# Experts of a routed layer: unsplit 4-byte products on column halves instead of three products of split parts

## The chip, the core and the metric

The kernel runs on one core of one Trainium2 chip. The time is that of one execution on the device in microseconds (us), and of several runs the median counts. One execution was recorded by the hardware profiler; all rows below are from it. TensorE multiplies matrices, ScalarE and VectorE work on elements, GpSimd works on elements more slowly and issues the indirect transfers (gathers and scatters by row), and SyncE issues the plain transfers. In rows, PE is TensorE, PEld its weight loads, ACT is ScalarE, DVE is VectorE, POOL is GpSimd, SP is SyncE; a q behind a name is that engine's sequencer.

## The reference

One layer of a decoder trunk on 1024 tokens of width 1024, all in 4-byte floats: a normalisation with a scale and shift made from a conditioning vector, one input projection, a gated linear recurrence in one branch, an attention over selected keys in the other, a gated merge and an output projection. The change touches what follows, a layer of routed experts:

```
g_sel = argmax(x @ w_group + b_group)                    # one of 4 groups
e_top = top 2 of 8 experts of that group
hid   = silu(xb @ w1[e]) * (xb @ w3[e])                  # 1024 -> 512
y     = hid @ w2[e]                                      # 512 -> 1024
out   = sum over the token's two experts of gate * y
```

Each of the 32 experts holds two 1024x512 weights and one 512x1024 weight, 6 MiB in all (6.29 MB). Every token goes to two experts, so an expert sees 64 tokens on the average, and how many it sees is known only while the kernel runs. The layer's result, scaled by a row, is added to the residual stream, and a last normalisation gives the output.

## The kernel before, in words

The trunk is one program in which stages follow one another: the input projection, the key selection, the recurrence, the attention, the merge, the output projection with the routing (`project_out`), and the experts (`experts`, `expert`, `combine`). Up to the experts nothing changes but two small tables.

Routing ends with a table of slots: for each expert a column of 128 slots in `idx`, which holds the tokens' row numbers, and a column of gates. Slots without a token hold a number out of bounds, which the gather and the scatter skip. An expert with more than 128 tokens would be finished by `overflow`, which runs under a condition that all engines evaluate (lines 1614 and 1618); with at most 128 tokens everywhere it is skipped.

In `expert` the 128 slots' rows are gathered, turned by eight transposes on TensorE (`tr`, line 1483), and split: `hilo` makes a rounded part with ScalarE and the rest with VectorE (lines 97 and 98). The weights are split likewise after they have landed (`weights`, lines 1472 and 1474). A product of two split operands is three one-pass products on TensorE, high by high, high by low and low by high: 48 of 128x512 for the first two weights (line 1501, into `pa` and `pb`), 24 for the third (`mm3`, lines 137 to 139, into `py`), 72 in all. Between them stand the activation (line 1506), the gated product (line 1507) and four transposes of the hidden layer. At the end the rows are scaled by the gate and the residual's scale (line 1539) and scattered with an addition onto the stream in memory (line 1543). The last two experts are not scattered; `combine` adds them by a product with a matrix of ones and zeros, and normalises.

The weights come as six transfers of 1 MiB per expert, which SyncE issues in order (line 1380) into a ring of buffers (`ring_tile`). Eight of the ring's buffers exist from the merge on, so some loads are early; five more (`ring_b`) are added for the first part of the experts and later given up to the overflow's memory. SyncE waits with each load until the last reader of its buffer is done; in this kernel the readers are the two engines that split. Two sets of buffers, six for high parts and four for low ones of 4 KiB per partition, hold the split weights.

The order of work is that of a list of generators: `experts` steps the generators of two neighbouring experts in turn, so that one expert's third product stands between the other's first products and its transposes; the framework then may order instructions of an engine by its own priorities.

## Time and profile before

| | us |
|---|---|
| median of 3 runs | 1864.37 |
| lowest and highest | 1861.35, 1865.53 |
| the profiled execution | 1865.06 |
| its span, first to last instruction | 1863.3 |

The mean granted clock of TensorE was 0.984 of full speed. Over the span TensorE was busy 1759.3 us, weight loads 1456.1, VectorE 1439.9, ScalarE 1170.1, GpSimd 398.8. The transfers moved 366.85 MB. The slices of the page divide the span by 40, 46.6 us each; a digit is the busy share in tenths. In the timeline a matmul's length goes from its start to a modelled end, and neighbours overlap; the distance from start to start is what one costs. In the groups by line, "idle before" is the time that the engine stood still ahead of such an instruction, with what ended it.

### The profile page before, as it was taken

Reading aid. Unit: us, or ns where it says so; the run is one execution under the profiler, and the core shown is the slowest. Engines: PE = TensorE matmul, PEld = TensorE weight load, DVE = VectorE, ACT = ScalarE, POOL = GpSimd, SP = SyncE. Lnnn points to the kernel's source line nnn. Section 1 sums busy time; section 2 is a strip of 40 time slices with the busy share of each in tenths; the row PEclk is TensorE's granted clock in tenths of the full one; section 3 lists DMA queues with packets and bytes.
Section 4 is the critical chain, followed back from the end, with each engine's and each line's share of the span. In section 5 each row is a group of like instructions: output and inputs, shape, how many; then the busy total and the mean of one; then the engine's idle time right before and its main releaser. Section 6 shows DMA issues by size and latency. Waiting matters only on the chain. (4 is left out here: it accounts for less than half of the span.)

```text
span 1863.3 us, 24597 instructions
## 1 busy us (share of the span) xinstructions
PE 1759.3 (94%) x8532; PEld 1456.1 (78%) x8532; DVE 1439.9 (77%) x2393; ACT 1170.1 (63%) x1730; POOL 398.8 (21%) x249
## 2 busy tenths in 40 slices
PE   3999999997999999999999999979999999999995
PEld 2788877786777888999788877858888888788774
DVE  6688876697777766778524456569999999999998
ACT  6565677725676767888512113348888887777765
POOL 4101002210010001212000001033554544344134
PEclk9999999998999999999999999979999999999998
DMA  9213754322112212121738544369989999999994
GB/s 297 61 35 104 237 179 147 109 89 65 59 54 73 68 58 93 55 66 57 216 107 252 194 152 170 138 238 350 379 329 344 363 376 367 366 380 371 357 338 182
DMA packets 163738, 366.85 MB, mean 197 GB/s; under 512 B 17855, under 2 KB 107543, under 8 KB 139160
## 3 DMA queue, kind: packets, MB, share of 16 engines
q1 hardware_dynamic: 152112, 340.50, 51.3%
q0 software_dynamic: 10192, 19.99, 3.9%
q10 hardware_dynamic: 1304, 4.74, 0.6%
q8 instruction: 68, 1.11, 0.3%
q14 instruction: 62, 0.51, 0.1%
HBM read 326.90 MB, written 54.53 MB: 205 GB/s over the span
## 5 line engine op out<-in xcount | busy, mean ns | idle before, releaser
L1472 ACT ACTIVATE whi<-raw_w 128x1024 fp32r<-128x1024 f32 x384 | 395.6, 1057 | 107.8 <-DMA raw_w<-in_moe_w_dram 28.2
L1474 DVE TENSOR_TENSOR wlo<-raw_w,whi 128x1024 fp32r<-128x1024 f32 x382 | 447.9, 1220 | 13.1 <-ACT whi L1472 4.7
L139 PE MATMUL pj<-uhi,wlo_in 128*128 128x512 f32 (+2 forms) x784 | 302.8, 387 | 5.6 <-POOL wlo_in L128 4.2
L137 PE MATMUL pj<-uhi,whi_in 128*128 128x512 f32 (+2 forms) x784 | 304.3, 388 | 1.2 <-ACT gq L706 1.2
L138 PE MATMUL pj<-ulo,whi_in 128*128 128x512 f32 (+2 forms) x784 | 302.0, 385 | 0.0
L1543 POOL DMA_INDIRECT h_spill<-ye,idx x30 | 179.4, 5980 | 215.0 <-DVE ye L1539 202.2
L139 PEld LDWEIGHTS pj<-uhi,wlo_in 128*128 128x128 f32 (+1 forms) x784 | 146.4, 187 | 37.8 <-POOL wlo_in L128 6.4
L137 PEld LDWEIGHTS pj<-uhi,whi_in 128*128 128x128 f32 (+1 forms) x784 | 146.6, 187 | 32.1 <-ACT gq L706 2.4
L138 PEld LDWEIGHTS pj<-ulo,whi_in 128*128 128x128 f32 (+1 forms) x784 | 146.6, 187 | 29.9 <-issue 1.0
L654 ACT ACTIVATE junk_a<-B,nt 128x768 bf16<-128x768 f32 (+2 forms) x93 | 96.8, 1041 | 49.6 <-DVE nt L650 41.2
L1501 PE MATMUL pa<-whi,xh 128*128 128x512 f32 x256 | 103.3, 403 | 0.6 <-ACT xh L97 0.5
L138 PE MATMUL py<-wlo,hh 128*128 128x512 f32 x256 | 100.9, 394 | 2.7 <-DVE wlo L1474 2.7
L1501 PE MATMUL pa<-whi,xl 128*128 128x512 f32 x256 | 100.6, 393 | 0.5 <-DVE xl L98 0.5
L137 PE MATMUL py<-gh,whi_y 128*128 128x512 f32 x256 | 99.9, 395 | 1.1 <-ACT gh L97 1.1
L1501 PE MATMUL pb<-whi,xh 128*128 128x512 f32 x256 | 100.0, 391 | 0.4 <-ACTq L1618 0.4
L139 PE MATMUL py<-gh,wlo_y 128*128 128x512 f32 x256 | 100.4, 393 | 0.0
L138 PE MATMUL py<-gl,whi_y 128*128 128x512 f32 x256 | 100.2, 393 | 0.1
L139 PE MATMUL py<-whi,hl 128*128 128x512 f32 x256 | 100.0, 391 | 0.0
L137 PE MATMUL py<-whi,hh 128*128 128x512 f32 x256 | 99.8, 400 | 0.1
L1501 PE MATMUL pb<-whi,xl 128*128 128x512 f32 x256 | 99.7, 389 | 0.0
L128 POOL TENSOR_TENSOR wlo_in<-raw_in,whi_in 128x1024 fp32r<-128x1024 f32 (+1 forms) x20 | 50.3, 2515 | 230.4 <-ACT whi_in L127 230.4
L127 ACT ACTIVATE whi_y<-raw_y 128x1024 fp32r<-128x1024 f32 x16 | 17.0, 1062 | 104.5 <-PE py L138 98.6
(403 smaller groups left out, 4119.2 us busy)
## 6 DMA issues: line engine op xcount, KB each, us to landing
raw_w<-in_moe_w_dram SPq DMA_DIRECT2D x191, 1024.0 KB, 12.6
raw_in<-in_w_in_dram SPq DMA_DIRECT2D x50, 512.0 KB, 3.5
wm<-in_w_mod_dram SPq DMA_DIRECT2D x32, 512.0 KB, 4.7
sg_spill<-gq SPq DMA_DIRECT2D x16, 512.0 KB, 2.6
sg<-sg_spill SPq DMA_DIRECT2D x32, 256.0 KB, 3.2
wm<-in_w_mod_dram SPq DMA_DIRECT2D x24, 256.0 KB, 5.8
g_spill<-ge SPq DMA_DIRECT2D x10, 512.0 KB, 2.6
gr<-g_spill SPq DMA_DIRECT2D x10, 512.0 KB, 3.6
```

The lines of the kernel that those rows point to most:

```text
L127: nc.scalar.activation(hi[:, :n], raw[:, :n], AF.Copy)
L128: eng.tensor_tensor(lo[:, :n], raw[:, :n], hi[:, :n].bitcast(F32), op=OP.subtract)
L137: mm(ps, ah, bh, start=start, stop=False)
L138: mm(ps, ah, bl, start=False, stop=False)
L139: mm(ps, al, bh, start=False, stop=stop)
L654: nc.scalar.activation(junk_a[:, :n], self.B[j], AF.Sign, bias=nt[:, i : i + 1], accum_out=cnt[:, i : i + 1])
L1472: self.last_hi = nc.scalar.activation(hi, part, AF.Copy).ins
L1474: eng.tensor_tensor(lo, part, hi.bitcast(F32), op=OP.subtract)
L1501: nc.tensor.matmul(ps, a[:, kk, :], b[:, k * DE : (k + 1) * DE], start=kk == 0 and a is xh and b is hi, stop=kk == KT - 1 and b is lo,)
L1543: nc.gpsimd.indirect_dma_start(out=self.hd, out_offset=bass.IndirectOffsetOnAxis(ap=idx, axis=0), in_=ye, in_offset=None, bounds_check=S - ...
```

## The change

Tables and ring: the split buffers go, a third part of the ring (`ring_c`, five buffers) is kept to the end, and `ring_b`'s five serve five times each. Beside the slots' gates, the number of tokens of each expert is kept (`n_e`), and the gates are copied to both halves of the partitions.

Products: operands are unsplit 4-byte floats. The slots fall into two halves of 64 (g = 0, 1). For each half two weights are multiplied in turn: the result of the first lies on partitions 0 to 63 of a PSUM bank, that of the second on 64 to 127, so the two products use the two halves of the array's columns. In `first` the two weights are the two first ones of the expert, in `second` the two halves of the third. The second half of the slots stands under a condition on TensorE alone, which reads the expert's count and jumps over it where the expert has at most 64 tokens. The accumulators are cleared once at the start. The order of TensorE's instructions is fixed as written: first products of expert e, transposes of e + 1, second products of e - 1, transposes of e's hidden layer.

```diff
-X_TAGS = [("xh", D), ("xl", D), ("hid", DE), ("hh", DE), ("hl", DE), ("ye", D)]
+X_TAGS = [("xT", D), ("sil", D), ("hid", DE), ("hT", DE), ("ye", D)]
 AHEAD = 3
-NL = 4
 RM = 4
-RA, RB = 4 + RM, 5
-NW = 6
-RU = [-1, -1, -1, -1, -1, -1, -1, 6] + [3, 3, 4, 4, 4]
+RA, RB, RC = 4 + RM, 5, 5
+RU = [-1] * RA + [5] * RB + [-1] * RC
...
-        self.gate_l = hp.tile([P, NE], F32, name="gate_l")
+
+        self.gate_h = [hp.tile([P, NE], F32, name=f"gate_h{g}") for g in range(2)]
+        self.n_e = hp.tile([P, NE], I32, name="n_e")
...
+            nc.vector.tensor_copy(self.n_e, pn[:, :NE])
...
-            nc.scalar.activation(self.gate_l, R["gates"], AF.Copy)
+            for g in range(2):
+                self.both(self.gate_h[g], R["gates"][g * 64 : (g + 1) * 64, :])
+
+    def both(self, dst, src):
+
+        for f in range(2):
+            self.nc.scalar.activation(dst[f * 64 : (f + 1) * 64, :], src, AF.Copy)
...
-            xp.tile([P, 640], F32, name="pad_at", tag="pad")
-            mp = self.pool(st, "moe")
-            tp = self.pool(st, "moeps", bufs=2, space=PSUM)
-            for n, b in (("whi", NW), ("wlo", NL)):
-                mp.tile([P, D], F32R, name=f"{n}_at", tag=n, bufs=b)
+            tp = self.pool(st, "moeps", space=PSUM)
+            self.ph = [tp.tile([P, 512], F32, name=f"ph_{i}") for i in range(2)]
+            self.py = [tp.tile([P, 512], F32, name=f"py_{i}") for i in range(2)]
+            self.ring_c = self.pool(st, "ring_c")
+            for i in range(RC):
+                self.ring_c.tile([P, 2048], F32, name=f"rc_{i}", tag=f"rc{i}")
...
-            self.prefetch(RA + RB - self.seq)
+            for t in self.ph + self.py:
+                nc.vector.memset(t, 0.0)
+            self.prefetch(RA + RB + RC - self.seq)
...
-            for e in range(NE + 1):
-                step(e)
-                step(e - 1)
-                step(e)
-                start(e + 1)
-                step(e - 1)
+            for e0, e1 in ((0, OV + 1), (OV + 1, NE + 1)):
+                with self.as_traced((mybir.EngineType.PE,)):
+                    for e in range(e0, e1):
+                        step(e)
+                        start(e + 1)
+                        step(e - 1)
+                        step(e)
...
+    def expert(self, xp, e, xg, idx, gates, raws, count=None, scatter=True):
+
+
+
+        nc, tc = self.nc, self.tc
+        T = lambda n, e, shape: xp.tile(list(shape), F32, name=f"{n}_{e}", tag=n, bufs=2)
+        n = None
+        if count is not None:
+            n = nc.values_load(
+                count, engines=[mybir.EngineType.PE], min_val=0, max_val=S,
+                skip_runtime_bounds_check_because="a token counts once",
+            )
+
+        def turned(dst, src, n, name):
...
-                pt = tp.tile([P, 4, P], F32, name=f"pt{name}_{e}_{g}", tag="pt")
+                pt = self.mmp.tile([P, 4, P], F32, name=f"pt{name}_{e}_{g}", tag="mm")
                 for k in range(4):
                     nc.tensor.transpose(pt[:, k, :], v[:, g + k, :], self.ident)
-                self.hilo(dst_h[:, g : g + 4, :], dst_l[:, g : g + 4, :], pt)
-
-        xh, xl = T("xh", e, (P, KT, P), F32R), T("xl", e, (P, KT, P), F32R)
-        tr(xh, xl, xg, KT, "x")
+                nc.scalar.activation(dst[:, g : g + 4, :], pt, AF.Copy)
+
+        def halves(product):
+            product(0)
+            with nullcontext() if n is None else tc.If(n > 64):
+                product(1)
+
+        xT = T("xT", e, (P, KT, P))
+        turned(xT, xg, KT, "x")
         yield
+        raws = iter(raws)
+        w = [[next(raws)() for _ in range(2)] for _ in range(2)]
+
+        def first(g):
+            for k in range(KT):
+                for f in range(2):
+                    nc.tensor.matmul(
+                        self.ph[g][f * 64 : (f + 1) * 64, :], xT[:, k, g * 64 : (g + 1) * 64],
+                        w[k // 4][f][:, (k % 4) * DE : (k % 4 + 1) * DE], start=k == 0, stop=k == KT - 1,
+                    )
+
+        halves(first)
+        sil, hid = T("sil", e, (P, 2, DE)), T("hid", e, (P, DE))
+        for g in range(2):
+            self.last_act = nc.scalar.activation(sil[64:P, g, :], self.ph[g][:64, :], AF.Silu).ins
+            nc.vector.tensor_tensor(hid[g * 64 : (g + 1) * 64, :], self.ph[g][64:P, :], sil[64:P, g, :], op=OP.mult)
         yield
+        hT = T("hT", e, (P, 4, P))
+        turned(hT, hid, 4, "h")
         yield
+        w2 = [next(raws)() for _ in range(2)]
+
+        def second(g):
+            for k in range(4):
                 for f in range(2):
+                    nc.tensor.matmul(
+                        self.py[g][f * 64 : (f + 1) * 64, :], hT[:, k, g * 64 : (g + 1) * 64],
+                        w2[k // 2][:, (k % 2) * D + f * 512 : (k % 2) * D + (f + 1) * 512], start=k == 0, stop=k == 3,
+                    )
+
+        halves(second)
         ye = T("ye", e, (P, D))
+        for g in range(2):
+            for f in range(2):
+                r, s_ = slice(f * 64, (f + 1) * 64), slice(f * 512, (f + 1) * 512)
+                nc.vector.scalar_tensor_tensor(
+                    ye[g * 64 : (g + 1) * 64, s_], self.py[g][r, :], gates[g][r, :], self.g2r[r, s_],
+                    op0=OP.mult, op1=OP.mult,
+                )
...
-        W = lambda n, i: mp.tile([P, D], F32R, name=f"fin_{n}{i}", tag=n, bufs=NW)
+        mp = xp
...
-        y = [(W("whi", 2 * i), W("whi", 2 * i + 1)) for i in range(2)]
+        y = [self.ring_tile(f"fin_y{i}", F32R).rearrange("p (z d) -> p z d", d=D) for i in range(2)]
+        y = [(v[:, 0, :], v[:, 1, :]) for v in y]
...
-        banks = [(tp, "py", 2), (tp, "py", 2), (tp, "pt", 2), (tp, "pt", 2)] + [(self.mmp, "mm", 3)] * 3
+        banks = self.ph + self.py + [None] * 3
...
+                    cs, cg = T("cs", (P, 1), I32), [T(f"cg{g}", (P, 1)) for g in range(2)]
+                    V.tensor_copy(cs, ls[:, ds(i, 1)])
+                    for g in range(2):
+                        for f in range(2):
+                            V.tensor_copy(cg[g][f * 64 : (f + 1) * 64, :], lg[g * 64 : (g + 1) * 64, ds(i, 1)])
```

In `combine` the split rows of the last two experts take two ring buffers, and the sums use the four accumulators. In `overflow` the gates are copied in the same way.

## Rows read from the trace of the kernel before

**Rows 1.** Page, busy tenths of TensorE and the DMA engines in 40 slices.

```profile
PE   3999999997999999999999999979999999999995
...
DMA  9213754322112212121738544369989999999994
```

**Rows 2.** Windows: length, busy PE, PEld, DVE, ACT, POOL; clock; DMA share.

```profile
1230.00:1240.00 10.00, 0.76 (x9) 0.65 (x9) 9.72 (x24) 1.76 (x2) 6.37 (x4) 0.62 0.38 132
1250.00:1550.00 300.00, 299.02 (x1407) 250.06 (x1407) 291.80 (x300) 243.06 (x269) 133.19 (x34) 1.00 0.96 353
1600.00:1800.00 200.00, 198.33 (x932) 164.05 (x931) 193.14 (x201) 151.95 (x177) 68.97 (x18) 1.00 0.99 371
```

**Rows 3.** Timeline of TensorE over one expert; start us, us, what, count.

```profile
1287.92 0.63 PE L1483 MATMUL pth<-ident,hid 128*128 128x128 f32 x4
1288.31 0.48 PE L1501 MATMUL pa<-whi,xh 128*128 128x512 f32 x1
...
1293.88 1.04 PE L1483 MATMUL ptx<-ident,xg 128*128 128x128 f32 x8
1294.67 0.48 PE L137 MATMUL py<-whi,hh 128*128 128x512 f32 x1
1294.99 0.39 PE L138 MATMUL py<-wlo,hh 128*128 128x512 f32 x1
...
1311.63 1.04 PE L1483 MATMUL ptx<-ident,xg 128*128 128x128 f32 x8
```

**Rows 4.** The same view at the stage's first and last products.

```profile
1249.89 0.79 PE L1501 MATMUL pa<-whi,xh 128*128 128x512 f32 x1
...
1252.93 0.40 PE L1501 MATMUL pa<-whi,xh 128*128 128x512 f32 x1
...
1829.77 0.39 PE L139 MATMUL py<-whi,hl 128*128 128x512 f32 x1
```

**Rows 5.** Waits of SyncE's queue from 1200 us: us in total, times, longest.

```profile
SPq L1380 <- DVE wlo L1474: 490.1, 175, 11.7
```

**Rows 6.** DMA queues from 1600 to 1800 us: packets, MB, share of engines.

```profile
q1 hardware_dynamic: 9552, 69.52, 89.4%
q0 software_dynamic: 2736, 4.54, 9.2%
```

**Rows 7.** Timeline of TensorE: 72-column, unsplit and 40-column products.

```profile
83.69 0.39 PE L138 MATMUL pj<-ulo,whi_in 128*72 128x512 f32 x1
83.91 0.40 PE L139 MATMUL pj<-uhi,wlo_in 128*72 128x512 f32 x1
84.15 1.88 PE L520 MATMUL pss<-csq,ones 128*128 128x512 f32 x4
...
1129.74 1.03 PE L1227 MATMUL plog<-wr,hT 128*128 128x40 f32 x8
```

**Rows 8.** Lines 1614 and 1618, TensorE queue: ns min/median/max, start us.

```profile
L1614 PEldq TENSOR_LOAD <-n_extra x1: 492/492/492, 1581.4 to 1581.4; - x1
...
L1618 PEldq COMPARE_BRANCH  x1: 450/450/450, 1582.0 to 1582.0; - x1
L1618 PEldq EVENT_SEMAPHORE  x1: 51/51/51, 1584.5 to 1584.5; - x1
```

**Rows 9.** Timeline of TensorE around that branch.

```profile
1584.05 0.39 PE L139 MATMUL py<-whi,hl 128*128 128x512 f32 x1
1584.59 0.47 PE L1501 MATMUL pa<-whi,xh 128*128 128x512 f32 x1
1584.90 0.40 PE L1501 MATMUL pa<-whi,xl 128*128 128x512 f32 x1
```

**Rows 10.** Groups by line from 1240 us: busy us, mean ns, idle before.

```profile
L1474 DVE TENSOR_TENSOR wlo<-raw_w,whi 128x1024 fp32r<-128x1024 f32 x382 | 447.9, 1220 | 13.1 <-ACT whi L1472 4.7 <-PE pa L1501 3.1 <-PE pb L1501 3.0
...
L1539 DVE SCALAR_TENSOR_TENSOR ye<-py,gate_l,modrow 128x512 f32<-128x512 f32 x62 | 43.5, 741 | 1.4 <-PE py L139 1.4
...
L1507 DVE TENSOR_TENSOR hid<-pb,hid 128x512 f32<-128x512 f32 x32 | 22.0, 689 | 5.4 <-PE pb L1501 5.4
```

More of the change, by code (lines that the diff above doesn't have):

```diff
@@ L1456, in gather @@
         )
-    def expert(self, xp, mp, tp, e, xg, idx, gate, raws, nw, scatter=True):
-        nc = self.nc
-        T = lambda n, e, shape, dt=F32: xp.tile(list(shape), dt, name=f"{n}_{e}", tag=n, bufs=2)
-        W = lambda n, e: mp.tile([P, D], F32R, name=f"{n}_{e}", tag=n, bufs=nw)
-        raws = iter(raws)
-        def weights(name):
-            raw = next(raws)()
-            for g in range(2):
-                hi, part = W("whi", f"{name}{g}"), raw[:, g * D : (g + 1) * D]
-                lo = mp.tile([P, D], F32R, name=f"wlo_{name}{g}", tag="wlo", bufs=min(nw, NL))
-                early = e == 0 and name[-1] == "0" and name[0] != "2"
-                eng = nc.gpsimd if e == 0 and name[0] == "1" and name[-1] == "0" else nc.vector
-                with self.tc.issue_after(self.rooted) if early else nullcontext():
-                    self.last_hi = nc.scalar.activation(hi, part, AF.Copy).ins
-                with self.tc.issue_after(self.listed) if early else nullcontext():
-                    eng.tensor_tensor(lo, part, hi.bitcast(F32), op=OP.subtract)
-                yield hi, lo
-        def tr(dst_h, dst_l, src, n, name):
+    def expert(self, xp, e, xg, idx, gates, raws, count=None, scatter=True):
[8 more added lines that the diff above has]
+        def turned(dst, src, n, name):
@@ L1487, in expert @@
-        tr(xh, xl, xg, KT, "x")
-        yield
-        pa = self.mmp.tile([P, 512], F32, name=f"pa_{e}", tag="mm")
-        pb = self.mmp.tile([P, 512], F32, name=f"pb_{e}", tag="mm")
-        for c in range(2):
-            if c:
-                yield
-            for ps, nm in ((pa, "1"), (pb, "3")):
-                for g, (hi, lo) in enumerate(weights(f"{nm}_{e}_{c}")):
-                    for b, As in ((hi, (xh, xl)), (lo, (xh,))):
-                        for k in range(2):
-                            kk = 4 * c + 2 * g + k
-                            for a in As:
-                                nc.tensor.matmul(
-                                    ps, a[:, kk, :], b[:, k * DE : (k + 1) * DE], start=kk == 0 and a is xh and b is hi,
-                                    stop=kk == KT - 1 and b is lo,
-                                )
@@ L1508, in expert @@
         yield
-        hh, hl = T("hh", e, (P, 4, P), F32R), T("hl", e, (P, 4, P), F32R)
-        tr(hh, hl, hid, 4, "h")
+        hT = T("hT", e, (P, 4, P))
+        turned(hT, hid, 4, "h")
         yield
-        final = e == NE - 1
-        pool, tag = (self.mmp, "mm") if final else (tp, "py")
-        py = [pool.tile([P, 512], F32, name=f"py_{e}_{f}", tag=tag) for f in range(2)]
-        def second(kk, f, hi, lo):
-            s_ = slice(f * 512, (f + 1) * 512)
-            self.mm3(py[f], hh[:, kk, :], hl[:, kk, :], hi[:, s_], lo[:, s_], kk == 0, kk == 3)
@@ L1678, in overflow @@
                     raws = [
-                        (lambda v=v, n=n: self.raw_load(op.tile([P, 2048], F32, name=n, tag="raw", bufs=1), v))
+                        (lambda v=v, n=n: self.raw_load(op.tile([P, 2048], F32, name=n, tag="raw", bufs=3), v))
                         for v, n in w
                     ]
-                    for _ in self.expert(xp, op, tp, "ov", xg, cs, cg, raws, 2):
+                    for _ in self.expert(xp, "ov", xg, cs, cg, raws):
                         pass
```

52 lines of the change are left out of this document (17 added, 35 removed).

## The prediction

> **What bounds the kernel now.** I read the page's slices first [rows 1]: TensorE is busy through nearly the whole span, and from about two thirds on the DMA engines are as full as TensorE. That last part is the expert stage, which is all that the change touches. Two stretches of it [rows 2]: from 1250 to 1550 us TensorE is busy 299.0 of 300 us at DMA share 0.96; from 1600 to 1800 us 198.3 of 200 us at share 0.99. VectorE stands at 97% of both. Three resources are nearly even, so an edit that relieves one of them is worth only its distance to the next.
>
> TensorE's own period is in the timeline [rows 3]: the eight transposes of one expert's input start at 1293.88 and the next expert's at 1311.63, 17.75 us. The transposes take 0.79 (to 1294.67) and 0.39 us (1287.92 to 1288.31); the other 16.57 us are 72 products, 0.23 us each with their hand-overs. 32 x 17.75 is 568 us; the stage runs from 1249.89 to about 1830 us [rows 4], 580 us, so 12 us of it are waits and a slow start (the usual pace is there only from 1252.93; I put this start at 2.5 us, an estimate that stands on both sides).
>
> The loads: SyncE waited 490 us for the splitting of weights (the buffers' last reader) before it could issue the next load [rows 5]. When the engines were full, from 1600 to 1800 us, 69.52 MB of weights landed beside 4.54 MB of gathers and scatters [rows 6]: 66.3 tiles of 1.0486 MB, 3.02 us each, 18.1 us for the six of an expert. So TensorE is the limit by a hair, and the loads come 0.35 us per expert behind it.
>
> **The change, part by part.**
>
> *Products.* 72 one-pass products become 24 unsplit ones for each half of 64 slots, in pairs on two halves of the columns. Running the reference's router on its inputs gives the tokens per expert: 15 experts have over 64 (102 88 68 84 71 80 101 101 100 77 67 79 94 69 68), 17 have fewer, none over 128. So 32 + 15 = 47 halves run, 47 x 24 = 1128 products. What one costs: the trace has an unsplit 128x512 product. The two on line 520 are four instructions, 1.88 us in all with 0.59 us for the last [rows 7], so they start 0.43 us apart, two to a product: 0.86 us. Are two at once really two at once? No row shows a product on half of the columns beside another. Bounds: serial, 1128 x 0.86 = 970 us; fully paired, 485 us. The nearest row speaks only of width: a product with 72 columns starts the next after 0.22 us just as one with 128 does [rows 7], so a narrow product alone saves nothing, and everything hangs on the pairing. I take 485 us: the two halves write different partitions and read different weights, and nothing they share is full in the rows, since an unsplit product moves 512 columns in 0.43 us where the present ones move them in 0.23.
>
> The Trainium skill (TensorE: Matmul & The Clock Gate, Packing small matmuls) has three column tiles measured at 2.38 times one, which would make my two somewhat under 2; the same section says that weight loads run beside running products only where the row groups differ, which column halves don't do. By that second rule the loads would stand between the products; this trace has no column halves to show it, and it is the first rival below.
>
> *Transposes.* Same number, 32 x (0.79 + 0.39) = 37.8 us. Four changes between transposes and products per expert, at the 0.09 us by which the product after the first one behind transposes is late (1294.67 to 1294.99, against 0.23) [rows 3]: 32 x 4 x 0.09 = 11.5 us. The Trainium skill (TensorEngine Tiling, Key Properties) says that a change of tiling mode drains TensorE; the drain that this trace has (next part, 0.4 us) in place of 0.09 would add 32 x 4 x 0.3 = 38 us.
>
> *The branches.* Two per expert, 64. The one branch in the trace [rows 8]: TensorE's queue loads the value (0.49 us), branches (0.45 us), and its next entry comes only at 1584.5, when the products before it have ended. The first product behind it starts 0.54 us after its predecessor and the next 0.31 us later [rows 9]: 0.4 us lost. The load and branch themselves lay under queued products. Taken as the price of each of the 34 skips, 13.6 us; where the second half runs nothing is jumped over, so I take half, 30 x 0.2 = 6 us. Bounds for a skip: nothing, to the 2.5 us from the branch at 1582.0 to 1584.5 with no cover, 85 us.
>
> *ScalarE and VectorE.* The splits go: 382 of 1.22 us on VectorE [rows 10] and their first halves on ScalarE. In come two gated products per expert at 0.69 us instead of one, four scaled rows at 0.74 instead of two. VectorE then works under 5 us per expert and leaves the path. The hidden layer's chain behind the last product (an activation and the 0.69 us of the gated product, some 1.4 us) lies under the next transposes and the 3.4 us of the second product that stands between. The clearing of four accumulators and the copies of the gates lie beside the gather, which TensorE awaits at the stage's start anyway.
>
> *Sum for TensorE.* 485 + 37.8 + 11.5 + 13.6 + 6 + 2.5 (slow start as now) = 556.4 us, against 568 + 2.5 today. An expert of one half takes 6.9 + 3.4 + 1.2 + 0.4 + 0.8 = 12.6 us, of two halves 22.4.
>
> *Loads.* These two lengths stand on either side of the 18.1 us that an expert's weights need. The ring grows from 13 to 18 tiles, then 13 instead of 8; memory freed by the split buffers. Of the first sixteen experts eleven are long: TensorE sets the pace and the ring is full. Experts 16 to 24 are nine short ones, 9 x 12.6 = 113 us of products for 54 tiles, 54 x 3.02 = 163 us. Of a full ring some 8 tiles are ahead of use, 24 us. So TensorE waits about 26 us there, less 2 for the expert before, 24. Bounds: no wait if the deeper queue raises the rate to 2.5 us per tile; 40 us if no lead is left. While it waits the granted clock may fall: it was 0.62 in the ten us after 1230, when TensorE had 0.8 us of work [rows 2]. At half of the clock a group of products for two tiles takes 6.9 us where its load takes 6.0, so the loss corrects itself; I leave it at nothing, up to 10 us.
>
> *Start and end.* The first product waits for a copy of all the transposed input, 0.8 us later than now (an estimate by the 0.69 us of a pass over 512 elements [rows 10] and its hand-over). At the end two scaled rows of 0.74 and the split stand behind the last product where today it is a little less: +1.4 us.
>
> Sum: 556.4 + 24 = 580.4 against 580.0, and 0.8 + 1.4: 2.6 us longer. The profiled execution took 1865.06 us (span 1863.3), 0.7 above the median of 1864.37. I forecast 1867 us: no gain, because the skipped halves are given back by long experts that TensorE bounds and short ones that the loads bound.
>
> **The rivals.**
>
> *Weight loads are not hidden, or the pairing is partial.* For: four loads per pair instead of two, and products of 40 columns start 0.11 us apart whatever their width (eight in 1.03 us) [rows 7], which is a load of 128 columns, so some 0.06 for 64. Against: the unsplit products of today hide theirs. If 0.06 to 0.11 stands in each instruction, 1128 x 0.06 to 0.11 = 68 to 124 us, less up to 24 of waits that vanish: 1911 to 1967 us. A pairing worth 1.5 instead of 2 adds 162 - 24 = 138: 2005. It decides from 0.001 us per instruction on, since the forecast stands 1.1 us below the bound for slower.
>
> *No pairing at all.* 485 us more, less the 24: 2328 us. For: the strict spacing of every product in the trace. Against: the two products share neither a weight nor a partition of the result.
>
> *A dear branch.* With 2 us uncovered per skip, 34 x 1.6 = 54 us, partly inside the waits for loads: 1890 to 1900.
>
> *Faster.* The wait for loads shrinks and the branches hide. For: the 3.02 us [rows 6] were taken with buffers that came free late; the new ring is 5 tiles deeper. With 2.8 us per tile, skips at 0.3 and free entries: 24 - 12, 13.6 - 10.2, 6 - 3, and 0.05 less at each hand-over (6): about 24 us less, 1843. Against: all must hold together, and TensorE alone would still need 540 us.
>
> *The skip doesn't act* (counts not seen as I computed): 17 x 10.3 = 175 us less 24, 2018. Unlikely; few experts lie near 64.
>
> **How the numbers follow.** Forecast, pairing holds and the sum is right within its bounds (1846 to 1895): 0.46, of which 0.15 falls below and 0.11 within 0.2% of today. That 0.2%, under 4 us, is about what a measurement of this kernel can tell from no change. Faster rival 0.14; loads not hidden or partial pairing 0.18; dear branch or inactive skip 0.05; no pairing 0.17. Faster 0.15 + 0.14 = 0.29, kept at 0.30; same 0.11; slower the rest, 0.59. The range leaves out the serial case and the rare ends: 1840 to 2030 us.
>
> **What would show it.** Pairing: two products of line `first` starting together or a pair every 0.86 us; four 0.43 apart in sequence would kill the forecast. Branches: gaps of 0.3 to 0.5 us behind each skip. Loads: TensorE idle for raw weights in experts 16 to 24 and hardly before, the DMA share under 0.95 in the first sixteen. VectorE under 30% in the stage. The forecast is wrong if periods differ from 12.6 (18.1 where load-bound) and 22.4 us, or the waits total far from 24.

## The result, and the profile after

The changed kernel takes 1885.95 us (median of 4 runs, 1884.63 to 1891.29) against 1864.95 us for the kernel before beside it (1861.35 to 1867.93): a ratio of 1.0119, 95% interval 1.0092 to 1.0146. That is slower by 1.2%, and 19 us above the predicted 1867.

The page of the changed kernel, in 40 slices, against [rows 1]: busy tenths of TensorE, of VectorE and of the DMA engines.

```profile
PE   3999999998999999999999989969999999888995
...
DVE  6689877696776768778433456531222212221227
...
DMA  9213754322212222121748444288989969999984
```

Windows of the expert stage, with the columns of [rows 2] (length, busy PE, PEld, DVE, ACT, POOL, granted clock, DMA share, GB/s):

```profile
1250.00:1600.00 350.00, 340.58 (x1624) 126.58 (x1626) 75.97 (x104) 52.03 (x93) 46.49 (x36) 0.99 0.89 336
1600.00:1730.00 130.00, 109.78 (x486) 40.07 (x482) 32.10 (x44) 21.43 (x39) 19.35 (x15) 0.96 1.00 389
1730.00:1850.00 120.00, 115.00 (x546) 42.77 (x542) 31.35 (x43) 19.26 (x34) 19.65 (x12) 1.00 0.86 326
```

VectorE has gone from 97% to 22% (75.97 of 350 us). TensorE and the loads now take turns: until 1600 TensorE is nearly full and the DMA engines stand at 0.89, from 1600 to 1730 it is the other way round, and after that TensorE leads again.

TensorE over one short expert's first product and the long expert's second product behind it, as in [rows 3]:

```profile
1292.70 0.75 PE L1492 MATMUL pth<-ident,hid 128*128 128x128 f32 x4
1293.37 7.09 PE L1509 MATMUL ph<-raw_w,xT 128*64 128x512 f32 x32
1301.17 1.13 PE L1492 MATMUL ptx<-ident,xg 128*128 128x128 f32 x8 [0.71 <-PEq L1497]
1302.24 7.09 PE L1528 MATMUL py<-raw_w,hT 128*64 128x512 f32 x32
```

A product of the program is two instructions in the rows, as in [rows 7]. The 32 instructions of a short first product take 6.88 us, 0.43 per pair: they run two at a time, as the rows of both TensorE queues show for a second product.

```profile
1603.78 3.65 PE L1528 MATMUL py<-raw_w,hT 128*64 128x512 f32 x16
...
1604.26 0.14 PEld L1528 LDWEIGHTS py<-raw_w,hT 128*64 128x64 f32 x2 [0.29 <-issue]
1604.69 0.14 PEld L1528 LDWEIGHTS py<-raw_w,hT 128*64 128x64 f32 x2 [0.29 <-issue]
```

Sixteen instructions in 3.65 us, and two loads of weights every 0.43 us, each 0.14 us long and out of sight. From start to start a long first product takes 13.88 us (15 of them), a short one 7.80 to 7.81 (17); a long second 7.02, a short one 3.96; the input's transposes 1.07, the hidden layer's 0.66 (medians). Two prices stand in these. The transposes took 0.79 and 0.39 before, so each group costs 0.27 to 0.28 more. A short first product has 6.88 us of pairs and takes 0.92 more, a short second one 3.44 and takes 0.52 more: these are the skips (the 0.71 us of idle time behind the branch, line 1497). About 0.13 us of each stands behind long products too (13.88 and 7.02 us for 13.76 and 6.88 of pairs), so the skips alone cost 0.80 and 0.38.

The stage's first and last products, as in [rows 4]:

```profile
1251.29 1.97 PE L1492 MATMUL ptx<-ident,xg 128*128 128x128 f32 x8 [10.52 <-DMA xg<-n_spill,idx]
1253.19 13.32 PE L1509 MATMUL ph<-raw_w,xT 128*64 128x512 f32 x58
...
1840.80 7.09 PE L1528 MATMUL py<-raw_w,hT 128*64 128x512 f32 x32
1847.82 0.97 PE L1594 MATMUL ph<-fin_y,fin_one 128*128 128x512 f32 x3
```

Between the profiled executions (1884.63 and 1865.06 us, 19.6 apart) the first product starts 3.3 us later (1253.19 against 1249.89), the stage is 14.5 us longer (594.6 from 1253.19 to 1847.82, against 580.1 with the 0.23 us of the last product), and 1.8 us come behind it.

TensorE's waits from 1240 us on: us in total, times, the longest.

```profile
PE ptx L1492 <- PEq L1497: 12.4, 17, 0.9
PE ptx L1492 <- DMA xg<-n_spill,idx: 10.5, 1, 10.5
PE ph L1509 <- DMA raw_w<-in_moe_w_dram: 6.9, 4, 1.9
PE ph L1509 <- DVEq L1622: 6.1, 1, 6.1
```

The waits for loads are listed as 6.9 us; products that start late one by one hide much of the rest. They are read better from stretched products. TensorE's timeline at experts 24 and 25:

```profile
1688.24 1.07 PE L1509 MATMUL ph<-raw_w,xT 128*64 128x512 f32 x2
1691.09 9.08 PE L1509 MATMUL ph<-raw_w,xT 128*64 128x512 f32 x30 [1.77 <-DMA raw_w<-in_moe_w_dram]
...
1706.55 1.07 PE L1509 MATMUL ph<-raw_w,xT 128*64 128x512 f32 x2
1709.54 3.94 PE L1509 MATMUL ph<-raw_w,xT 128*64 128x512 f32 x16 [1.92 <-DMA raw_w<-in_moe_w_dram]
```

The first of these products takes 12.63 us from start to start and the second 19.28, 4.8 and 5.4 above their usual length. All such excess at experts 23 to 25 adds up to 14.1 us. Not all of it is waiting: from 1691.0 to 1694.3 us, behind a wait, the granted clock was 0.57, which makes up some 1.7 us of expert 24's excess.

The 6.1 us is one stall, at the branch around the overflow blocks (line 1622) behind expert 18. Rows around it:

```profile
1607.58 3.04 DVE L1538 SCALAR_TENSOR_TENSOR ye<-py,gate_h,modrow 64x512 f32<-64x512 f32 x4 [3.40 <-PEq L1497]
...
1607.74 0.72 PE L1492 MATMUL pth<-ident,hid 128*128 128x128 f32 x4 [0.31 <-PEq L1497]
...
1614.53 1.97 PE L1509 MATMUL ph<-raw_w,xT 128*64 128x512 f32 x4 [6.06 <-DVEq L1622]
```

TensorE has nothing behind 1608.5 and starts again at 1614.53, with its products at half the pace for 5.2 us; the window there shows the granted clock at 0.50 (1.2 of 2.4 GHz):

```profile
1614.50:1619.70 5.20, 5.17 (x13) 1.66 (x15) 0.00 (x0) 0.00 (x0) 0.00 (x0) 0.50 1.02 399
```

Stall and slow stretch make 8.7 us (6.1 and 2.6). The same branch cost 0.4 us before [rows 9]. What TensorE waits for is VectorE's queue, which goes on 6.1 us after its own branch, 3.8 us after its last sum (1610.62); TensorE's own queue has passed at 1608.7. Line 1622 of the changed kernel, then line 1618 of the kernel before, with the columns of [rows 8]:

```profile
L1622 DVEq COMPARE_BRANCH  x1: 72/72/72, 1608.2 to 1608.2; - x1
L1622 DVEq EVENT_SEMAPHORE  x1: 21/21/21, 1614.4 to 1614.4; - x1
```

```profile
L1618 DVEq COMPARE_BRANCH  x1: 72/72/72, 1585.2 to 1585.2; - x1
L1618 DVEq EVENT_SEMAPHORE  x1: 21/21/21, 1590.9 to 1590.9; - x1
```

So VectorE's queue took 5.6 us to pass before the change too; there TensorE went on at 1584.59 without it.

The queue of the weights from 1600 to 1800 us, as in [rows 6] (packets, MB, share): 70.82 MB, 67.5 tiles, 2.96 us each against 3.02.

```profile
q1 hardware_dynamic: 9726, 70.82, 87.9%
```

### The profile page after: what moved, and what is told of

The parts are those of the page before. It is cut to its first block, busy times and chain, and to the rows that moved or that the text cites. A ratio compares the mean times of both kernels' runs of the same rounds, so it can differ in the third digit from the quotient of the medians.

```text
span 1882.7 us, 23253 instructions
## 1 busy us (share of the span) xinstructions
PE 1749.7 (93%) x8484; PEld 1189.0 (63%) x8484; DVE 1018.7 (54%) x2018; ACT 803.7 (43%) x1379; POOL 238.5 (13%) x245
## 5 line engine op out<-in xcount | busy, mean ns | idle before, releaser
L1509 PE MATMUL ph<-raw_w,xT 128*64 128x512 f32 x1504 | 339.8, 602 | 13.2 <-DMA raw_w<-in_moe_w_dram 6.9
L1509 PEld LDWEIGHTS ph<-raw_w,xT 128*64 128x64 f32 x1504 | 107.2, 138 | 221.8 <-issue 205.3
L1518 DVE TENSOR_TENSOR hid<-ph,sil 64x512 f32<-64x512 f32 x64 | 44.4, 694 | 316.9 <-ACT sil L1517 315.9
L1538 DVE SCALAR_TENSOR_TENSOR ye<-py,gate_h,modrow 64x512 f32<-64x512 f32 x128 | 96.0, 750 | 150.3 <-PE py L1528 95.0
L1517 ACT ACTIVATE sil<-ph 64x512 f32<-64x512 f32 x64 | 34.3, 583 | 330.6 <-PE ph L1509 203.7
L1528 PE MATMUL py<-raw_w,hT 128*64 128x512 f32 x752 | 168.6, 596 | 0.0
L1528 PEld LDWEIGHTS py<-raw_w,hT 128*64 128x64 f32 x752 | 51.0, 137 | 94.0 <-issue 88.8
L1545 POOL DMA_INDIRECT h_spill<-ye,idx x30 | 47.4, 1581 | 240.0 <-DVE ye L1538 226.3
L125 ACT ACTIVATE whi_in<-raw_in 128x1024 fp32r<-128x1024 f32 (+1 forms) x51 | 53.3, 1045 | 46.3 <-PE pj L136 40.9
L618 DVE TENSOR_SCALAR_CACHE_REDUCE junk<-B,trial 128x384 bf16<-128x384 f32 (+2 forms) x93 | 69.2, 744 | 1.9
```

The lines of the kernel that those rows point to most:

```text
L125: nc.scalar.activation(hi[:, :n], raw[:, :n], AF.Copy)
L618: nc.vector.tensor_scalar(junk[:, :n] if dst is None else dst, src, thr_ap, 0.0, op0=op, op1=OP.add, accum_out=out,)
L1509: nc.tensor.matmul(self.ph[g][f * 64 : (f + 1) * 64, :], xT[:, k, g * 64 : (g + 1) * 64], w[k // 4][f][:, (k % 4) * DE : (k % 4 + 1) * DE] ...
L1518: nc.vector.tensor_tensor(hid[g * 64 : (g + 1) * 64, :], self.ph[g][64:P, :], sil[64:P, g, :], op=OP.mult)
L1528: nc.tensor.matmul(self.py[g][f * 64 : (f + 1) * 64, :], hT[:, k, g * 64 : (g + 1) * 64], w2[k // 2][:, (k % 2) * D + f * 512 : (k % 2) * ...
L1538: nc.vector.scalar_tensor_tensor(ye[g * 64 : (g + 1) * 64, s_], self.py[g][r, :], gates[g][r, :], self.g2r[r, s_], op0=OP.mult, op1=OP.mult,)
```

## The experiments

Each time below is a median, where no single run is named. Gains are differences of medians; by the ratios to the kernel before, which ran beside each, they come out some 2 to 3 us larger, and two ratios less than about 0.003 apart are not told apart. Theory: pairing holds, TensorE's time per expert is what the sum says plus dearer turns and skips, and the loads take over only at experts 23 to 25. Rivals stand with each run.

### Neighbours on one half of the columns

```diff
-            for k in range(KT):
-                for f in range(2):
+            for f in range(2):
+                for k in range(KT):
```

(and the same in `second`)

> The products of one column half are issued all together and then those of the other half, so that neighbours in TensorE's program share a half of the columns; the work is the same. Theory (two products run at once because neighbours in program order lie on different halves): of the 564 pairs at 0.86 us each only the one neighbouring product at each change of half can still pair, so the products alone grow from 485 to about 950 us, the load waits (14 us) go, and the kernel takes about 2335 us (2290 to 2370). Rival (TensorE finds the free half by itself, over more than its next instruction): within 5 us of the changed kernel's 1886.

Measured: 2150.5 us (one run), between the two. A long first product took 22.63 us, a long second one 8.90. TensorE's two queues at the start of a second product:

```profile
1308.89 5.05 PE L1528 MATMUL py<-raw_w,hT 128*64 128x512 f32 x18
...
1309.38 0.14 PEld L1528 LDWEIGHTS py<-raw_w,hT 128*64 128x64 f32 x1 [0.29 <-issue]
1309.81 0.14 PEld L1528 LDWEIGHTS py<-raw_w,hT 128*64 128x64 f32 x1 [0.29 <-issue]
1310.23 0.14 PEld L1528 LDWEIGHTS py<-raw_w,hT 128*64 128x64 f32 x1 [0.29 <-issue]
1310.66 0.19 PEld L1528 LDWEIGHTS py<-raw_w,hT 128*64 128x64 f32 x3 [0.29 <-issue]
```

One load per 0.43 us for the first four instructions of the eight, then two at a time while the other half's first four run beside the last four of these, and so on. Run one after another the 32 instructions would take 13.76 us; three changes of half give back 13.76 - 8.90 = 4.86 us, 1.6 each, 3.8 instructions. The long first product gives the same: 27.52 - 22.63 = 4.89 us for its three changes, although its runs are twice as long. So both theories missed: the pairing is not tied to direct neighbours, and TensorE doesn't look over the whole product. It reaches about four instructions ahead: in the rows the loads go in twos from the fifth instruction on. The order in the changed kernel, k outside and f inside, is well within that and pairs everything.

### No skip

```diff
-            with nullcontext() if n is None else tc.If(n > 64):
-                product(1)
+            product(1)
```

> Both halves of every expert are multiplied, without the branches and the loads of counts. Theory (a skip costs TensorE 0.92 us at the first matrix and 0.52 at the second, a branch not used about 0.13): every expert takes 2 x 6.88 + 2 x 3.44 for products and about 1.7 for transposes, 22.4 us, in all 32 x 22.4 = 716 us against the 568 of the changed kernel; its load waits (14) go, the stall at the overflow branch stays: about 1886 + 148 - 14 = 2020 us (2005 to 2035), with long experts' first stretch 0.1 shorter. Rival (the skip's price is a wait that would have come anyway, for hidden layer or loads): transposes become dearer by as much where no branch stands before them, and the time is above 2040.

Measured: 2028.1 us (one run), inside the theory's 2005 to 2035. TensorE's timeline in one period:

```profile
1296.78 13.95 PE L1508 MATMUL ph<-raw_w,xT 128*64 128x512 f32 x64
1310.66 1.16 PE L1492 MATMUL ptx<-ident,xg 128*128 128x128 f32 x8
1311.75 7.09 PE L1527 MATMUL py<-raw_w,hT 128*64 128x512 f32 x32
```

The first product takes 13.88 us here without any branch, as it does in the changed kernel with one: a half that is run pays nothing for its branch. The transposes cost the same, 1.09 and 0.67, so the 0.27 us per group belongs to the change of shape and not to the branches. All skips together are worth 142 us, 8.4 for each of the 17 short experts (10.3 of products less 1.44 of skips, less what went to waits).

### The floor of the loads

```diff
-            with nullcontext() if n is None else tc.If(n > 64):
-                product(1)
```

> The second halves are left out everywhere (the slots from 64 on are not computed), and with them the branches: 12 us of TensorE's time per expert against 18.1 us of loads. This measures the floor that the loads of the weights set. Theory (loads are close behind TensorE in the changed kernel: 24 us between the two at most): the stage is bound by the loads, some 174 tiles from its start at 2.95 to 3.02 us each, 513 to 525 us, so about 1805 to 1830 us in all. Rival (the loads only seem full because the ring keeps them busy, and could go faster): under 1790.

Measured: 1840.3 us (one run), 10 above the theory's end. The window of the first experts, and TensorE's waits for loads at the first product (those at the second add 3.0 us):

```profile
1250.00:1600.00 350.00, 298.05 (x1252) 109.08 (x1252) 86.45 (x119) 60.64 (x106) 52.76 (x41) 0.95 0.99 371
```

```profile
PE ph L1507 <- DMA raw_w<-in_moe_w_dram: 78.6, 42, 3.0
```

With TensorE's work cut to 12 us per expert the DMA share is 0.99 from the start. No gain on TensorE alone can go far below 1840; the kernel before is 25 us above that, the changed one 46.

### No overflow branch

```diff
-                    self.overflow(xp)
```

> The call of the overflow blocks is left out (with these inputs its branch is never taken, so nothing of the result changes). Theory (TensorE's stall of 5.6 us there, and the 2.6 us at a lower clock behind it, come from the branch that all engines pass together, where VectorE comes late): the stall goes, about 1877 us (1874 to 1880) where TensorE's time shows through to the end. Rival (the loads are next behind TensorE, so that the 8.7 us return as waits for loads at experts 22 to 25): within 2 us of 1886. The ring of buffers still falls from 18 to 13 there, as in the changed kernel.

Measured: 1886.5 us, ratio to before 1.0115 (1.0097 to 1.0133): the rival. The stall is gone from the list of waits, and in its place:

```profile
PE ph L1508 <- DMA raw_w<-in_moe_w_dram: 12.5, 7, 2.1
```

Read from the stretched products, the waits for loads are 22.3 us instead of 14.1, from expert 21 on: 8.2 of the 8.7 us came back. The stall looked like the largest single wait inside the stage and is worth nothing there, because the loads are the limit behind it.

### Loads behind the first gather

The router's end: the products that list the gates start at 1238.86 us, 5.6 us earlier than before (1244.47), and yet the first expert's product is 3.3 us later. In the changed kernel five loads of the ring are issued from 1227.3 on and five more around 1242, in front of and beside the last write of normed rows (issued at 1233.5) and the gather that reads it (1242.7). The loads' line, ns and first and last start as in [rows 8]:

```profile
L1390 SPq DMA_DIRECT2D raw_w<-in_moe_w_dram x10: 327/422/753, 1227.3 to 1243.7; - x10
```

Two experiments.

```diff
-            self.prefetch(RA + RB + RC - self.seq)
             for e in range(AHEAD - 1):
                 self.gather(xgs[e], self.idx[:, e : e + 1])
+            self.held = True
+            self.prefetch(RA + RB + RC - self.seq)
...
+            if getattr(self, "held", False):
+                self.nc.gpsimd.memset(t[:, 0:1], 0.0)
```

> The ring's loads that the changed kernel issues ahead of the first gathers (its pool takes up 14 of the 18 tiles there) are issued behind them: a one-column write by GpSimd into each of these tiles, behind the gathers in its queue, holds them back. Theory (the stage starts 3.3 us later than before, though the router's last step is 5.3 us earlier, because these loads now run in front of the write and the gathers of the normed rows; once the ring is full in the long experts at the start, loads follow the buffers that come free, so a shift of the start carries through to the end): first product at about 1245.5 instead of 1253.2, and about 1878.5 us (1876 to 1881). Rival (the loads set the end, and holding them back costs them what the start gains): first product earlier, but load waits at experts 22 to 25 grow by as much, 1886 or above.

Measured: 1889.7 us, ratio to before 1.0121 (1.0102 to 1.0139). The edit missed its aim: five of the one-column writes came at 1229.2 us, ahead of the last rows' write (1235.4), and the other five ahead of the gathers. So the loads went out early as before, and the rows' write took 9.2 us to land:

```profile
raw_w<-in_moe_w_dram SPq DMA_DIRECT2D x10, 1024.0 KB, 13.1
...
n_spill<-u ACTq DMA_DIRECT2D x1, 512.0 KB, 9.2
```

It says nothing about either theory. The second takes the order from data:

```diff
+            self.held = xgs[0]
+            self.prefetch(RA + RB + RC - self.seq)
...
+            if getattr(self, "held", None) is not None:
+                self.nc.gpsimd.tensor_copy(t[:, 0:1], self.held[:, 0:1])
```

> As the run that wanted the ring's loads behind the first gathers, but by data: a column of each of the ten tiles is copied from the first gathered rows, so that none of these loads can be issued before that gather has landed. (In the run before, five of them were still issued at 1229.3, ahead of the last rows' write, which again took 9.2 us, where the kernel before has 2.7.) Theory (these loads in front of the write and the gather cost the start of the stage about 7 us): write 3 us, gather about 4.5 us, first product some 6 to 7 us earlier against the router's end, and, since the ring is full again in the long experts, the time falls by 4 to 7 us, 1879 to 1882. Rival (20 us of loads held back are missing later): first product earlier, waits for loads at experts 1 to 4 or 22 to 25 that grow by as much, 1886 to 1895.

Measured: 1876.3 us, ratio to before 1.0055 (1.0040 to 1.0069): 9.6 us less than the changed kernel and below even the theory's range. The write lands in 2.7 us:

```profile
n_spill<-u ACTq DMA_DIRECT2D x1, 512.0 KB, 2.7
```

TensorE's timeline shows the first expert 6.0 us behind the gates (1244.41 to 1250.43; 14.3 in the changed kernel, 5.4 before):

```profile
1244.41 1.92 PE L1361 MATMUL gates<-rg,perm 128*128 128x32 f32 x8 [1.34 <-DVE rg L1355]
1248.53 1.97 PE L1497 MATMUL ptx<-ident,xg 128*128 128x128 f32 x8 [2.21 <-DMA xg<-n_spill,idx]
1250.43 14.66 PE L1514 MATMUL ph<-raw_w,xT 128*64 128x512 f32 x64
```

(This execution was the slowest of the six, some 5 us late already at the router's last row write, 1232.5 against 1226.9, and so its times count by their distances.) Loads held back by 20 us are made up: the DMA share from 1250 to 1600 is 0.93 instead of 0.89.

### A later overflow branch, and a deeper ring

```diff
-RU = [-1] * RA + [5] * RB + [-1] * RC
-OV = 18
+RU = [-1] * RA + [10] * RB + [-1] * RC
+OV = 30
```

> The overflow branch goes from behind expert 18 to behind expert 30, so that the ring keeps its 18 tiles until then (5 of them are given up at the branch). Theory (waits of 14 us for loads at experts 22 to 25, which took back the stall in the run without overflow blocks, come from a ring of 13 that cannot hold the loads that long experts allow for the short ones behind them): these waits fall below 3 us, the stall of 5.6 us moves to the end of the stage, and 1872 us (1868 to 1876). Rival (the loads themselves are late there whatever the ring's depth): waits at about the same experts and 1882 to 1886; with the stall now at a place where nothing hides it, up to 1892.

Measured: 1882.1 us, ratio to before 1.0082 (1.0066 to 1.0098), the lower end of the rival's range. The waits for loads lie between the two: they fall from 14.1 to 10.0 us (4.0, 0.6 and 5.4, at experts 24 and 25). The stall and the slow stretch behind it stand at the end, 5.4 and 2.4 us, where nothing hides them. The ring's depth is part of the waits; that the rate of the loads is the rest was not tested by itself.

The same with the branch in front of expert 29's second product, the loop written as a list of steps that is cut there:

```diff
+            todo = [(w, e) for e in range(NE + 1) for w in ('first', 'start', 'second', 'turn')]
+            cut = 4*OV + 2
+            for part in (todo[:cut], todo[cut:]):
```

> As the run with the overflow branch behind expert 30 and a ring of 18 until then, but the branch stands in front of the second product of expert 29, not behind it. Theory (TensorE's stall at the branch is the time that VectorE needs for the four weighted sums of the second product, 3.0 us, and that GpSimd and VectorE then need to pass the branch; in front of that product VectorE has only the gated product of the first to finish): the stall falls from 5.5 to 1 to 2.5 us and the 2.4 us at a lower clock go, about 1876 us (1873 to 1879), against 1882. Rival (the stall is the passing of the branch by all engines, whatever work is before it): 5 us again, 1882.

Measured: 1882.2 us (1881.0 to 1882.3), ratio 1.0082 (1.0069 to 1.0096): the rival. VectorE had only the hidden layer to finish, and TensorE waited as long:

```profile
PE py L1530 <- DVEq L1624: 5.6, 1, 5.6
```

So it isn't VectorE's four weighted sums: its queue again goes on only 5.4 us after its branch (1804.9 to 1810.4), and TensorE 0.1 us behind it. In this run GpSimd was late too, at two operations of `combine` until 1809.97; in the changed kernel it had passed at 1611.7, 2.7 us before VectorE. The stall is the passing of the branch by VectorE's queue; what that queue does in these 5 to 6 us stays open.

### Turns side by side

```diff
                         step(e)
-                        start(e + 1)
                         step(e - 1)
+                        start(e + 1)
                         step(e)
```

> TensorE's order within a period is changed: the input's transposes for the next expert stand directly in front of the hidden layer's, behind the second product, so that the array's shape changes twice in a period and not four times. Theory (each change of shape between products on 64 columns and transposes on 128 lets the array run empty, 0.28 us a group): transposes together 1.46 us instead of 1.73 per expert, 8.6 us over 32; what experts 18 to 25 gain goes to load waits, so about -6: 1880 us (1877 to 1883). Rival (0.28 us is the price of each product on one half of the columns behind a transpose, or the first product now waits for the copy of the transposed input): no gain, 1885 to 1890, with ph's wait for xT above 0.2 us each.

Measured: 1880.9 us, ratio to before 1.0074 (1.0058 to 1.0091), 5.1 less than the changed kernel: the theory. TensorE's timeline around a short expert:

```profile
1311.18 1.16 PE L1492 MATMUL ptx<-ident,xg 128*128 128x128 f32 x8
1312.18 0.65 PE L1492 MATMUL pth<-ident,hid 128*128 128x128 f32 x4
1312.75 7.09 PE L1509 MATMUL ph<-raw_w,xT 128*64 128x512 f32 x32
1320.20 3.65 PE L1528 MATMUL py<-raw_w,hT 128*64 128x512 f32 x16 [0.36 <-PEq L1497]
```

Transposes take 1.57 us from start to start (1311.18 to 1312.75) instead of 1.73, less of a gain than the theory's 1.46; long products take 0.05 to 0.10 less each (13.78 and 6.97). A short first product takes 7.40 us instead of 7.80, but a short second one 4.36 instead of 3.96: the load of the next expert's count goes with the input's transposes, and so it now stands in view behind the second product's skip. The first product's wait for the copied input doesn't show.

### The count loaded later

```diff
             product(0)
+            if n is None and count is not None:
+                n = nc.values_load(
```

> The load of an expert's count from SBUF into a register of TensorE's sequencer is moved from the front of the input's transposes to between the products of the first half and the branch behind them. Theory (the load, 0.30 us, is exposed where it stands, since behind a skip nothing is queued; behind 32 queued products it is hidden): the skip's price at the first matrix falls from 0.92 to about 0.6 us; 17 x 0.3, of which experts 18 to 25 return theirs, so -3 to -5: 1882 us (1880 to 1884). Rival (the sequencer runs only four instructions ahead of the array, 0.9 us, as the run with the halves one after the other shows, so that the load and the branch together eat that lead): no gain at skips, and 0.1 to 0.3 us more at each branch taken: 1886 to 1890.

Measured: 1884.7 us, ratio to before 1.0096 (1.0079 to 1.0112). The time lies between the theory's range and the rival's and is not told from the changed kernel's. At the skip the theory holds: 7.40 us instead of 7.81 for a short first product.

```profile
1299.37 7.09 PE L1510 MATMUL ph<-raw_w,xT 128*64 128x512 f32 x32
1306.77 1.13 PE L1487 MATMUL ptx<-ident,xg 128*128 128x128 f32 x8 [0.31 <-PEq L1498]
```

So a skip costs 0.52 us at either product, and 0.4 of the 0.92 was the load of the count, which had nothing queued in front of it. Of 17 x 0.41 = 7 us less on TensorE the median shows 1.2; the waits for loads rose from 14.1 to 19.3.

### Together

The loads held back by data, the turns and the count, with the branch behind expert 24 and a ring of 19 tiles, and the same with the branch and ring as in the changed kernel:

```diff
-NXG = 4
+NXG = 3
-RA, RB, RC = 4 + RM, 5, 5
-RU = [-1] * RA + [5] * RB + [-1] * RC
-OV = 18
+RA, RB, RC = 4 + RM, 5, 6
+RU = [-1] * RA + [8] * RB + [-1] * RC
+OV = 24
```

> Everything together that gained by itself: loads behind the first gather (-9.6), the transposes of input and hidden layer side by side (-5), the count loaded behind the first half's products (-1), the overflow branch behind expert 24, where TensorE waits for loads anyway, so that the ring stays whole through the short experts, and a ring of 19 tiles (a gather buffer less). Theory (TensorE's share of a period and the lag of the loads at experts 22 to 25 are the two limits; the first falls by some 0.5 us an expert, the second by six tiles more in the ring): waits for loads below 9 us, the branch's 5 us hidden in them, and 1855 us (1850 to 1862), below the kernel before's 1866. Rival (the loads are the limit from expert 15 on and take back TensorE's gains): 1866 to 1872, with waits for loads of 15 us or more.

> As the kernel with everything together, but with the overflow branch behind expert 18 again and the ring of 18 and then 13 tiles: what TensorE's three gains are worth without the larger ring. Theory (what TensorE gains in experts 16 to 25 goes to waits for loads): -7 against the run with only the loads held back, 1869 us (1866 to 1873), load waits of 15 to 25 us. Rival (the ring's size doesn't matter): the same as the kernel with everything together, within 3 us.

Measured: 1863.4 us (ratio to before 0.9989, 0.9977 to 1.0000) and 1871.1 us (1.0029, 1.0019 to 1.0038). The second lies within its theory; the larger ring and the later branch together are worth 7.7 us (no run has one without the other here). The first lies 8 us above its forecast, between the theory's range and the rival's, level with the kernel before and 22.6 us under the changed one. Its window of the first experts:

```profile
1250.00:1600.00 350.00, 344.10 (x1670) 131.90 (x1668) 80.34 (x110) 50.39 (x95) 48.11 (x37) 1.00 0.98 379
```

Both resources are now full up to 1600 (TensorE 98%, DMA share 0.98). The waits for loads, 16.5 us from the stretched products of experts 22 to 24, are as long as the rival had them, and the branch's stall and slow stretch, some 6 us, lie beside them and not in them.

## Why the prediction was right, and where its number was not

The side was right (slower, given 0.59), and the time lies in the likeliest case's own range, 1846 to 1895. Part of that is luck: of the 0.59, 0.35 stood on partial or no pairing, which the rows rule out, 0.05 on a dear branch or a skip that doesn't act, and only some 0.20 on the case that came, whose own forecast was no gain. By its steps:

- *Products, 485 us.* Exact: 1128 products in pairs at 0.86 us, 15 x (13.76 + 6.88) + 17 x (6.88 + 3.44) = 485.0. The first rival falls: two loads of 0.14 us lie under each pair on the same rows, and nothing of them shows. The Trainium skill (TensorE: Matmul & The Clock Gate, Packing small matmuls) says that weight loads run beside products only where row groups differ; this trace differs, and the measurement decides. (That rival's 68 to 124 us counted 1128 loads; two to a product, the rows have 2256, so its price would have been twice that.)
- *Transposes with their hand-overs, 49.3 us.* Measured 54.5, without the first expert's input, which is turned before the first product. The prediction took 0.09 us for a change, from products on the whole array [rows 3]; on column halves both groups of an expert cost 0.27 us more. The Trainium skill (TensorEngine Tiling, Key Properties) says that a change of tiling mode drains TensorE, and the trace agrees in that a group costs more only between products on column halves, at 0.27 us a group, less than the 0.4 per change that the prediction set beside it. That this is a drain is not shown by itself.
- *Branches.* A half that is run: 3.9 us of gaps where 6 stood, and none of it by the branch. A skip was put at 0.4 us from one branch [rows 9], 13.6 us for 34, and measured 0.52, plus 0.4 for the count's load at the first: 24.5 us. The prediction said that load and branch lie under queued products, as at [rows 8]; behind a skip nothing is queued. Counted so, this is the term that was mis-sized most, by 10.9 us. Without the 0.13 us that stands behind every product, run or skipped, a skip costs 0.38 us at the second product, which is the prediction's 0.4, and 0.80 at the first. Then the skips are 20.1 us, 6.5 over, which is about the count's load (7); the halves that run cost nothing for their branch, 6 under; and the turns are 62.9 us, 13.6 over. The sum is the same: a change of shape was priced too low, and the load of the count was taken to be out of sight.
- *Sum for TensorE.* 567.9 us regular time instead of 553.9: +5.2 - 2.1 + 10.9 = +14.0. That is the same as 32 periods of before (568), so what the products gained was spent on turns, skips and the width of long experts. By the sign that the prediction gave itself, an expert of two halves takes 22.6 us (22.4 forecast) and one of one half 13.5 (12.6): the short one is where it was off.
- *Load waits, 24 us.* 14.1, but with 8.7 of stall and slow clock in the same stretch: 22.8 together, and 22.3 where the stall was taken out. The step was right, place included (experts 23 to 25, behind the short ones that the prediction named), and the stall, which it did not name, was free. (1.7 of the 14.1 are the lower clock, which the prediction left at nothing.)
- *Start.* The later first product was put at 0.8 us and came 3.3 us later, although the router ended 5.6 us earlier. This step failed: the prediction weighed the deeper ring in the stage, but not that its loads go out in front of the gather. Holding them back is worth 9.6 us, the largest gain of any single edit that keeps the work.
- *End.* +1.4 us; measured +1.8.

So inside the stage the mechanism was right: products halved in cost per half, long experts bound by TensorE and the last of the short ones by loads. At its start it was not. The sum's 2.6 us on the profiled execution of before make 1867.7, and the changed kernel's took 1884.6: of these 17 us the sum for TensorE has 14.0, the first and last steps inside the stage 1.4, its start 2.5 and its end 0.4, less 1.2 on load waits and stall. Such a sum isn't what an edit gives back, though: taking out 8.7 us of stall gave nothing, 7 us of skips gave 1.2 (not told from none), and holding back loads, 3.3 us late by the trace, gave 9.6.

## What to carry to other kernels

Where two limits take turns along a stage, walk through it in order with both before pricing an edit: time saved on the engine counts only where nothing behind it waits for the other limit. A freed buffer is a transfer issued earlier; ask which small transfer on the critical path it will now run in front of. A branch should be priced with what is queued before it, since loading its value was hidden under queued work here and in full view behind a skip.

## What the runs showed of the hardware

- TensorE pairs products on two column halves over some four instructions of its program: with runs of 8 and of 16 on one half, every change of half gave back 3.8 to 3.9 instructions of 0.43 us, and the other half's loads begin beside the fifth of eight.
- At the branch that all engines pass, VectorE's queue went on 5.3 to 6.8 us after its own branch in all runs with it but two (3.5 with half of the products, 2.9 with the branch behind expert 24), whether VectorE was at the weighted sums or not, and 5.6 in the kernel before. Where its next product waited for that queue, TensorE stood 5.3 to 7.0 us in the changed kernel's order of work (3.7 with half of the products) and 4.0 and 4.4 with turns side by side. Behind expert 24 it stood 2.9 us, for its own queue. In the kernel before, where it waited for neither, the branch cost 0.4.
- Behind that stall TensorE ran at the lower clock (0.50 granted), which cost 1.4 to 3.0 us; in the changed kernel 2.6 us after 6 us without work.
- A 512 KB write landed in 2.7 us with no load issued in the 4 us before it (the kernel before and the run with loads held back by data), and in 8.1 to 9.2 us in the eight runs in which its landing was recorded behind five loads of 1 MB.
